# Another first stage for one transformer block: whole-row token tiles, another load order, another pass order

## The chip, the cores and the metric

The kernel runs on one core of one Trainium2 chip. Its time is the device time of one execution in microseconds (us). The kernel before takes 1711.54 us, the median of three runs (1708.84 to 1712.44). The profile is of one more execution, which took 1710.46 us.

## The reference: what is computed

One layer works on 256 latent tokens `x` and 256 context tokens `ctx`, all float32, model width 2048. The first stage computes the beginning of it: a modulated RMS norm of both token sets, times the columns of `w_in` that give keys and values.

```
m_lat = adaln(c,     w_ada, b_ada)      # silu(c) @ w_ada + b_ada, six chunks of 2048: shift, scale, ...
m_ctx = adaln(c_ctx, w_ada, b_ada)
hc = rms_norm(ctx, norm1_g) * (1 + m_ctx[1]) + m_ctx[0]
h  = rms_norm(x,   norm1_g) * (1 + m_lat[1]) + m_lat[0]
pc = hc @ w_in[:, :3072]                # keys and values of the context tokens
p  = h  @ w_in                          # keys, values, queries and gates of the latent tokens
...                                     # grouped-query and differential attention, gates, two projections
x  = x + gate * ((silu(h2 @ w_ff_gate) * (h2 @ w_ff_up)) @ w_ff_down)
```

## The kernel before, in words

**Numbers.** Every float32 product is made of three passes on TensorE: each operand is split into a high part (rounded, `hi`) and a low part (the rest, `lo`), and hi x hi, hi x lo and lo x hi are added in PSUM. For a weight tile ScalarE makes the high part (line 227, tile `whi`) and VectorE, once GpSimd, the low part (line 229, tile `wlo`).

**Keys and values in steps.** The 2048 rows of `w_in` are worked off in six steps of 1, 1, 2, 4, 4 and 4 row tiles of 128. A step needs the shift and scale of its rows for both token sets. `ada_cond` makes them from the array `ada_t`, the columns of `w_ada` in an order that suits the steps: it loads 512 KB pieces (line 282, tile `wada`), multiplies them on TensorE with the conditioning vectors (line 290), copies the sums out (line 294, `asb`), turns them (line 299, `atp`) and ends on VectorE (lines 302 to 309). Step 0 and step 1 have four such pieces each, step 2 has eight.

**Step 0, where the change lies.** There are four groups of 128 tokens: 2 and 3 are `x`, 0 and 1 are `ctx`. They are worked in the order 2, 3, 0, 1. For each one `row_norm` sums the squares of a 128x2048 row block (four quarters: two on ScalarE at line 128, two on VectorE at line 130), adds up the partial sums (line 133) and takes the power -1/2 on GpSimd (line 134). `row_scale` multiplies the first 128 columns by the result (line 139). `mod_first` turns these 128 columns on TensorE (line 355, `xtp`), and makes the modulated high part on ScalarE (line 360) and the low part on VectorE (lines 361 and 362). `kv_first` multiplies with five column groups of 512 of the first weight rows: groups 2 and 3, then 4 and 5, then 0, so 15 matmuls per token group, 60 in all (lines 370, 371 and 373), and copies the sums out (lines 378 and 380). Column group 1 follows apart (`group_1`, lines 233 to 235). `keep_busy` puts transposes of the identity into TensorE's queue (line 345) that compute nothing of use.

**Then.** `spread_rstd` spreads the four norms over the partitions (line 152). From step 1 on, rows come turned from DRAM (`tok_t`, line 162), `modulated` makes both parts (lines 331 to 335), and the matmuls of lines 233 to 235 run in one stream. Attention, the output projection and the feed-forward part follow, with the same three-pass matmuls.

**What sets the order.** The code is written in the order of the work, and a list scheduler of the language orders each engine's instructions from it by its own estimates; `issue_after` holds an instruction behind another. All large loads are issued by one queue, SP, strictly in order. An SP load waits until its buffer is free: weights and `wada` pieces share a ring of seven 4 KB-per-partition buffers (`wraw`), taken in order. At most eight loads are under way, since the ninth reuses the semaphore of the first.

## Time and profile before

| | before |
|---|---|
| median of three runs | 1711.54 us (1708.84 to 1712.44) |
| the profiled execution | 1710.46 us |
| its span from first to last instruction | 1708.7 us |
| TensorE busy (PE) | 1682.3 us, 98% |
| TensorE weight load (PEld) | 1354.0 us, 79% |
| VectorE busy (DVE) | 1148.3 us, 67% |
| ScalarE busy (ACT) | 769.8 us, 45% |
| GpSimd busy (POOL) | 202.2 us, 12% |
| DMA | 413.15 MB, mean 242 GB/s |
| granted TensorE clock | 0.998 of full |

Of the profiled time 1.8 us lie outside the span. A row of a timeline gives the start in us from the beginning of the span, the time busy, the engine, the line, the operation, the tile written and the tiles read, how many instructions were merged, and in brackets how long the engine had been idle and what ended it. "SPq" rows are load issues. Float32 matmuls of `wada` and transposes are run as two instructions each, so that counts in the trace are twice those of the program there.

### The profile page before, as it was taken

The numbers are of one execution on the slowest core, as the hardware profiler recorded it, in microseconds if no ns is written. First come the engines' busy times: TensorE is split into PE (matmuls) and PEld (weight loads), VectorE is DVE, ScalarE is ACT, GpSimd is POOL, SyncE is SP. The second block draws the span as 40 slices with busy tenths as digits, with TensorE's granted clock in tenths as the row PEclk, the third lists the DMA queues.
The fourth block names the chain that finished last, engine by engine and source line by source line (L and its number), as shares of the span: only waits on it lengthen the run. The fifth ranks groups of instructions, "written<-read, shape, count | busy, mean of one in ns | idle before, by whom it ended". The sixth has DMA issues, their size and how long they took to land.

```text
span 1708.7 us, 21517 instructions
## 1 busy us (share of the span) xinstructions
PE 1682.3 (98%) x7889; PEld 1354.0 (79%) x7889; DVE 1148.3 (67%) x1459; ACT 769.8 (45%) x1045; POOL 202.2 (12%) x296
## 2 busy tenths in 40 slices
...
GB/s 285 304 295 267 265 333 175 210 259 259 251 179 220 223 224 282 231 246 206 244 272 237 295 173 222 222 271 264 266 270 265 266 275 255 237 219 191 219 205 91
DMA packets 181291, 413.15 MB, mean 242 GB/s; under 512 B 15008, under 2 KB 16240, under 8 KB 180928
## 3 DMA queue, kind: packets, MB, share of 16 engines
...
## 4 chain that ended last, share of the span: by engine, by line
PE 87%; DVE 5%; DMA 3%; ACT 2%; issue 2%; POOL 1%; SPq 0%; ACTq 0%; DVEq 0%; POOLq 0%
PE mm L233 26%; PE mm L234 26%; PE mm L235 26%; PE ada L290 2%; DVE wlo L229 1%; PE ptp L764 1%; ACT whi L227 1%; DMA wraw<-in_w_in_dram 1%; PE o L785 1%; PE s L740 1%; ACT p L689 1%; DMA fturn<-turn_d 0%; DMA tok<-in_x_dram 0%; DVE nr L479 0%; DMA gate_d<-gate 0%
## 5 line engine op out<-in xcount | busy, mean ns | idle before, releaser
L229 DVE TENSOR_TENSOR wlo<-wraw,whi 128x1024 fp32r<-128x1024 f32 x497 | 606.6, 1222 | 420.2 <-ACT whi L227 419.3
L227 ACT CAST whi<-wraw 128x1024 fp32r<-128x1024 f32 x498 | 523.0, 1051 | 729.1 <-PE mm L235 606.3
L234 PE MATMUL mm<-wlo,hT 128*128 128x512 f32 x684 | 266.2, 389 | 0.8 <-DVE wlo L229 0.8
L233 PE MATMUL mm<-whi,hT 128*128 128x512 f32 x684 | 266.2, 389 | 0.0
L235 PE MATMUL mm<-whi,hT 128*128 128x512 f32 x684 | 266.1, 389 | 0.0
L233 PE MATMUL mm<-whi,xT 128*128 128x512 f32 x630 | 251.8, 403 | 1.5 <-ACT xT L334 0.7
L234 PE MATMUL mm<-wlo,xT 128*128 128x512 f32 x630 | 247.1, 392 | 1.1 <-DVE wlo L229 1.0
L235 PE MATMUL mm<-whi,xT 128*128 128x512 f32 x630 | 246.1, 391 | 0.0
L431 DVE SCALAR_TENSOR_TENSOR ada<-wada,vt,ada 128x1024 f32<-128x1024 f32 x120 | 152.1, 1278 | 0.0
L234 PEld LDWEIGHTS mm<-wlo,hT 128*128 128x128 f32 x684 | 128.4, 188 | 27.6 <-DVE wlo L229 1.1
L233 PEld LDWEIGHTS mm<-whi,hT 128*128 128x128 f32 x684 | 128.4, 188 | 26.9 <-ACT whi L227 0.3
L235 PEld LDWEIGHTS mm<-whi,hT 128*128 128x128 f32 x684 | 128.4, 188 | 26.8
L233 PEld LDWEIGHTS mm<-whi,xT 128*128 128x128 f32 x630 | 117.7, 188 | 39.2 <-issue 13.1
L234 PEld LDWEIGHTS mm<-wlo,xT 128*128 128x128 f32 x630 | 118.5, 188 | 26.1 <-DVE wlo L229 2.9
L235 PEld LDWEIGHTS mm<-whi,xT 128*128 128x128 f32 x630 | 118.3, 188 | 25.2
L233 PE MATMUL mm<-whi,fT 128*128 128x512 f32 x354 | 137.5, 388 | 0.5 <-DVE y L1083 0.5
L234 PE MATMUL mm<-wlo,fT 128*128 128x512 f32 x354 | 137.3, 388 | 0.0
L235 PE MATMUL mm<-whi,fT 128*128 128x512 f32 x354 | 137.3, 388 | 0.0
L233 PEld LDWEIGHTS mm<-whi,fT 128*128 128x128 f32 x354 | 66.4, 188 | 15.3 <-issue 0.8
L235 PEld LDWEIGHTS mm<-whi,fT 128*128 128x128 f32 x354 | 66.4, 188 | 13.8
L234 PEld LDWEIGHTS mm<-wlo,fT 128*128 128x128 f32 x354 | 66.5, 188 | 13.5
L233 PE MATMUL mm<-whi,oT 128*128 128x512 f32 x192 | 75.9, 396 | 0.0
...
## 6 DMA issues: line engine op xcount, KB each, us to landing
wraw<-in_w_in_dram SPq DMA_DIRECT2D x159, 512.0 KB, 5.0
wada<-in_w_ada_dram SPq DMA_DIRECT2D x128, 512.0 KB, 4.7
wraw<-in_w_ff_gate_dram SPq DMA_DIRECT2D x88, 512.0 KB, 4.4
wraw<-in_w_ff_up_dram SPq DMA_DIRECT2D x88, 512.0 KB, 5.3
wraw<-in_w_ff_down_dram SPq DMA_DIRECT2D x88, 512.0 KB, 4.4
wada<-in_ada_t_dram SPq DMA_DIRECT2D x64, 512.0 KB, 5.9
wraw<-in_w_br_a_dram SPq DMA_DIRECT2D x32, 512.0 KB, 5.0
wraw<-in_w_out_dram SPq DMA_DIRECT2D x32, 512.0 KB, 5.3
```

The source lines that it names most:

```text
L227: last_hi.append(nc.scalar.copy(out=hi[:, 0:nk], in_=raw[:, 0:nk]))
L229: last_lo.append((by or nc.vector).tensor_tensor(out=lo[:, 0:nk], in0=raw[:, 0:nk], in1=hi[:, 0:nk].bitcast(F32), op=ALU.subtract))
L233: nc.tensor.matmul(ps, lhsT=ah, rhs=wh, start=first, stop=False, skip_group_check=skip)
L234: nc.tensor.matmul(ps, lhsT=ah, rhs=wl, start=False, stop=False, skip_group_check=skip)
L235: return nc.tensor.matmul(ps, lhsT=al, rhs=wh, start=False, stop=last, skip_group_check=skip)
L290: last_pe[0] = nc.tensor.matmul(aps[32 * g:32 * g + 32, 0:ncol], lhsT=cst[:, k, :], rhs=rhs, start=(k < 4), stop=(k >= NKT - 4))
L431: nc.vector.scalar_tensor_tensor(out=dst, in0=wt, scalar=sc[:, 0, kt:kt + 1], in1=dst, op0=ALU.mult, op1=ALU.add)
L689: nc.scalar.activation(out=p, in_=sp, func=AF.Exp, bias=mx, accum_out=rs)
L740: nc.tensor.matmul(sps[i], lhsT=qT[rows, x, hh, tk * P:(tk + 1) * P], rhs=kT["b", grp][y][rows, hh, :], start=(n == 0), stop=(n == 2))
L764: nc.tensor.transpose(out=tp[:, kt * P:(kt + 1) * P], in_=p[:, kt * P:(kt + 1) * P], identity=ident)
L785: nc.tensor.matmul(op[:, 0:BV], lhsT=pT[:, kt, :], rhs=vb[:, kt, hh * BV:(hh + 1) * BV], start=(kt == 0), stop=(kt == 3))
```

## The change

The change touches the first stage alone.

- A token group's 2048 columns lie in one tile per group, loaded as two pieces of 128x1024; before, a quarter of the columns of all groups shared a tile and each group came in four pieces of 128x512.
- Token group 2 is loaded ahead of the four `wada` pieces of step 0; the weights of column groups 2 to 5 follow them, then group 3, the weights of column group 0, and the context groups.
- The squares: ScalarE takes the middle 1024 columns in one instruction, VectorE the first and the last 512. All but the first 512 columns are written over in place.
- Group 2 is normed and turned before the conditioning of step 0 is computed; the turning is a step of its own (`turn_first`). `keep_busy` stands at three places with six transposes each, before at two with eight and six.
- All low parts of weights are made on VectorE. Group 2's own modulation stands ahead of the weight splits on VectorE.
- In `kv_first` the pass with the low part of the weights comes last; before, the pass with the low part of the tokens did.
- For group 3 the leftover column group 0 of group 2 comes first.

**Place 1: SP's queue at the start.** `head` holds the conditioning vectors, `wada` the conditioning pieces, `tok` the token tiles, `wraw` the weights, `tok_t` the turned tokens of the later steps. Before:

```order
L88 DMA head<-in_head_dram 80x128
L282 DMA wada<-in_ada_t_dram 128x1024 x4
L101 DMA tok_92<-in_x_dram 128x512
L101 DMA tok_93<-in_x_dram 128x512
L101 DMA tok_94<-in_x_dram 128x512
L101 DMA tok_95<-in_x_dram 128x512
L208 DMA wraw<-in_w_in_dram 128x1024 x2
```

and, behind the context tokens:

```order
L216 DMA wraw<-in_w_in_dram 128x2x512
L162 DMA tok_t_408<-in_x_t_dram 128x2x384
L162 DMA tok_t_408<-in_ctx_t_dram 128x2x384
L282 DMA wada<-in_ada_t_dram 128x1024 x4
L208 DMA wraw<-in_w_in_dram 128x1024
```

Now:

```order
L102 DMA tok_92<-in_x_dram 128x1024 x2
L282 DMA wada<-in_ada_t_dram 128x1024 x4
L208 DMA wraw<-in_w_in_dram 128x1024 x2
L102 DMA tok_185<-in_x_dram 128x1024 x2
L208 DMA wraw<-in_w_in_dram 128x512
L102 DMA tok_190<-in_ctx_dram 128x1024 x2
L102 DMA tok_193<-in_ctx_dram 128x1024 x2
L216 DMA wraw<-in_w_in_dram 128x2x512
L282 DMA wada<-in_ada_t_dram 128x1024 x4
L208 DMA wraw<-in_w_in_dram 128x1024
L162 DMA tok_t_389<-in_x_t_dram 128x2x384
L162 DMA tok_t_389<-in_ctx_t_dram 128x2x384
```

Group 2's tokens moved ahead of step 0's four pieces, and step 1's four pieces ahead of the turned tokens.

**Place 2: TensorE from the last matmuls of token group 3 into the first context group.** `xT` is the modulated token part of `x`, `cT` that of `ctx`. Before:

```order
L373 MATMUL mm<-whi,xT_216 128x512 x4
L355 MATMUL xtp<-ident,tok_92 128x128
L370 MATMUL mm<-whi,xT_216 128x512
L371 MATMUL mm<-wlo,xT_216 128x512
L373 MATMUL mm<-whi,xT_216 128x512
L370 MATMUL mm<-whi,xT_216 128x512
L371 MATMUL mm<-wlo,xT_216 128x512
L373 MATMUL mm<-whi,xT_216 128x512
L370 MATMUL mm<-whi,cT 128x512
L371 MATMUL mm<-wlo,cT 128x512
```

Now:

```order
L374 MATMUL mm<-whi,xT_205 128x512
L375 MATMUL mm<-whi,xT_205 128x512
L377 MATMUL mm<-wlo,xT_205 128x512
L290 MATMUL ada<-wada,cst 32x128
L351 MATMUL xtp<-ident,tok_190 128x128
L290 MATMUL ada<-wada,cst 32x128 x8
L374 MATMUL mm<-whi,cT 128x512 x4
L290 MATMUL ada<-wada,cst 32x128 x4
L375 MATMUL mm<-whi,cT 128x512 x2
L377 MATMUL mm<-wlo,cT 128x512 x2
```

Thirteen of the 32 conditioning matmuls of step 1 moved from behind the context groups into the first of them, nine of these ahead of its first matmul; further on, 16 of them stand in and behind the second context group and 3 behind `group_1`. Of step 2's matmuls of 256 columns, 16 now stand ahead of the stream of step 1; before, eight did.

**Place 3: VectorE from the modulation of token group 3 on.** `vb` and `ka` are copies of sums out of PSUM. Before:

```order
L130 SCALAR_TENSOR_TENSOR junk,sums<-tok_93 128x512
L361 TENSOR_SCALAR hx<-xtp,mod_162,mod_134 128x128
L229 TENSOR_TENSOR wlo<-wraw,whi 128x512
L362 TENSOR_TENSOR xT_216<-hx,xT_216 128x128
L130 SCALAR_TENSOR_TENSOR junk,sums<-tok_95 128x512
L133 TENSOR_REDUCE sums<-sums 128x1
L139 TENSOR_SCALAR tok_92<-tok_92,sums 128x128
L378 COPY vb_106<-mm 128x512
```

Now:

```order
L365 TENSOR_SCALAR hx<-xtp,mod_177,mod_149 128x128
L366 TENSOR_TENSOR xT_205<-hx,xT_205 128x128
L229 TENSOR_TENSOR wlo<-wraw,whi 128x512
L133 SCALAR_TENSOR_TENSOR junk,sums<-tok_190 128x512
L382 COPY ka_101<-mm 128x512
L133 SCALAR_TENSOR_TENSOR tok_190,sums<-tok_190 128x512
L133 SCALAR_TENSOR_TENSOR junk,sums<-tok_193 128x512
L136 TENSOR_REDUCE sums<-sums 128x1
L382 COPY vb_105<-mm 128x512
L139 TENSOR_SCALAR tok_190<-tok_190,sums 128x128
```

Ahead of the scaling of the first context group (line 139) there now stand two copies of sums and one square of the second context group. Further on, inside step 2, two transposes of the conditioning stand about 24 matmuls later on TensorE; behind that every engine's order is the same in both kernels.

The diff:

```diff
--- before.py
+++ after.py
@@ -89,17 +89,20 @@
     warm = small("warm", 1)
     nc.scalar.activation(out=warm, in_=neghalf[:, 0:1], func=AF.Silu)
     sums = tab.tile([P, 24], F32, name="sums")
-    ssq, r_tok = sums[:, 0:20].rearrange("p (i q) -> p i q", i=4), sums[:, 20:24]
+    ssq, r_tok = sums[:, 0:16].rearrange("p (i q) -> p i q", i=4), sums[:, 20:24]
     nc.gpsimd.memset(sums, EPS)
-    tok_in = [big_tile(f"tok{q}").rearrange("p (i c) -> p i c", i=4) for q in range(4)]
+    tok_in = {}
     def load_tokens(src, i):
-        for q in range(4):
-            nc.sync.dma_start(out=tok_in[q][:, i, :], in_=src[0, i % 2 * P:(i % 2 + 1) * P, q * CG:(q + 1) * CG])
-
+        tok_in[i] = big_tile(f"tok{i}")
+        for h in range(2):
+            nc.sync.dma_start(out=tok_in[i][:, h * 2 * CG:(h + 1) * 2 * CG],
+                              in_=src[0, i % 2 * P:(i % 2 + 1) * P, h * 2 * CG:(h + 1) * 2 * CG])
+
+    load_tokens(t["x"], 2)
     nc.scalar.activation(out=head[0:32, :], in_=head[0:32, :], func=AF.Silu)
     hps = tp_ps("hps")
     nc.tensor.transpose(out=hps[:, 0:80], in_=head, identity=ident[0:80, 0:80])
@@ -120,22 +123,19 @@
         last_pow.append(nc.gpsimd.tensor_tensor(out=r, in0=r, in1=neghalf[:, 0:n], op=ALU.pow))
         return r
-    def row_norm(i):
-        for q in range(4):
-            xt = tok_in[q][:, i, :]
-            junk = scratch("junk", tag="p", bufs=4)
-            if q % 2 == 0:
-                nc.scalar.activation(out=junk, in_=xt, func=AF.Square, scale=D ** -0.5, accum_out=ssq[:, i, q:q + 1])
-            else:
-                nc.vector.scalar_tensor_tensor(out=junk, in0=xt, scalar=1.0 / D, in1=xt, op0=ALU.mult, op1=ALU.mult,
-                                               accum_out=ssq[:, i, q:q + 1])
+    def row_norm(i, late=None):
+        xt = tok_in[i]
+        mid, end = xt[:, CG:3 * CG], xt[:, 3 * CG:]
+        with tc.issue_after(late[0].ins) if late else nullcontext():
+            nc.scalar.activation(out=mid, in_=mid, func=AF.Square, scale=D ** -0.5, accum_out=ssq[:, i, 0:1])
+        with tc.issue_after(late[1].ins) if late else nullcontext():
+            for n, (src, dst) in enumerate(((xt[:, 0:CG], scratch("junk", tag="p", bufs=4)), (end, end))):
+                nc.vector.scalar_tensor_tensor(out=dst, in0=src, scalar=1.0 / D, in1=src, op0=ALU.mult, op1=ALU.mult,
+                                               accum_out=ssq[:, i, 1 + n:2 + n])
         r = r_tok[:, i:i + 1]
         nc.vector.tensor_reduce(out=r, in_=ssq[:, i, :], axis=AX.X, op=ALU.add)
         last_pow.append(nc.gpsimd.tensor_tensor(out=r, in0=r, in1=neghalf[:, 0:1], op=ALU.pow))
-        return r
-
-    def row_scale(i, r):
-        xt = tok_in[0][:, i, 0:P]
+        xt = xt[:, 0:P]
         nc.vector.tensor_scalar(out=xt, in0=xt, scalar1=r, scalar2=None, op0=ALU.mult)
     r_of = []
@@ -216,7 +216,7 @@
         nc.sync.dma_start(out=raw[:, 0:nk], in_=src[r0:r0 + nk * P, c0:c0 + CG].rearrange("(k p) c -> p k c", p=P))
         return split_w(raw, nk, in_big)
-    def split_w(raw, nk, in_big=False, late=None, by=None):
+    def split_w(raw, nk, in_big=False, late=None):
         if in_big:
             both = big_tile("wbig", F32R).rearrange("p (h k c) -> p h k c", h=2, c=CG)
             hi, lo = both[:, 0], both[:, 1]
@@ -226,7 +226,7 @@
         with tc.issue_after(late[0].ins) if late else nullcontext():
             last_hi.append(nc.scalar.copy(out=hi[:, 0:nk], in_=raw[:, 0:nk]))
         with tc.issue_after(late[1].ins) if late else nullcontext():
-            last_lo.append((by or nc.vector).tensor_tensor(out=lo[:, 0:nk], in0=raw[:, 0:nk], in1=hi[:, 0:nk].bitcast(F32), op=ALU.subtract))
+            last_lo.append(nc.vector.tensor_tensor(out=lo[:, 0:nk], in0=raw[:, 0:nk], in1=hi[:, 0:nk].bitcast(F32), op=ALU.subtract))
         return hi, lo
     def mm3(ps, ah, al, wh, wl, first, last, skip=False):
@@ -344,6 +344,12 @@
             for _ in range(n):
                 nc.tensor.transpose(out=idle[:, 0:P], in_=ident, identity=ident)
+    turned_first = {}
+
+    def turn_first(tok):
+        turned_first[tok] = tp_ps("xtp")[:, 0:P]
+        last_pe[0] = nc.tensor.transpose(out=turned_first[tok], identity=ident, in_=tok_in[tok][:, 0:P])
+
     def mod_first(tok):
         k0, nk = steps[0]
@@ -351,14 +357,12 @@
         w, c0 = (0, (tok - 2) * P) if tok >= 2 else (1, tok * P)
         if k0 not in cT_of:
             cT_of[k0] = big_tile("cT", F32R).rearrange("p (h k c) -> p h k c", h=2, c=CTX)
-        tp = tp_ps("xtp")
-        last_pe[0] = nc.tensor.transpose(out=tp[:, 0:P], identity=ident, in_=tok_in[0][:, tok, 0:P])
+        tp = turned_first[tok]
         hx = scratch("hx")[:, 0:P]
         v = xT.tile4(0) if w == 0 else cT_of[k0]
         hi, lo = [v[:, x, 0, c0:c0 + P] for x in range(2)]
-        with tc.issue_after(last_hi[-1].ins):
-            first_hi.append(nc.scalar.activation(out=hi, in_=tp[:, 0:P], func=AF.Identity, scale=scale[:, 0, w:w + 1], bias=shift[:, 0, w:w + 1]))
-        nc.vector.tensor_scalar(out=hx, in0=tp[:, 0:P], scalar1=scale[:, 0, w:w + 1], scalar2=shift[:, 0, w:w + 1], op0=ALU.mult, op1=ALU.add)
+        first_hi.append(nc.scalar.activation(out=hi, in_=tp, func=AF.Identity, scale=scale[:, 0, w:w + 1], bias=shift[:, 0, w:w + 1]))
+        nc.vector.tensor_scalar(out=hx, in0=tp, scalar1=scale[:, 0, w:w + 1], scalar2=shift[:, 0, w:w + 1], op0=ALU.mult, op1=ALU.add)
         last_first.append(nc.vector.tensor_tensor(out=lo, in0=hx, in1=hi.bitcast(F32), op=ALU.subtract))
         firsts[tok] = hi, lo
@@ -368,9 +372,9 @@
         for cg in cgs:
             wh, wl = ws0[cg]
             nc.tensor.matmul(ps[cg], lhsT=hi, rhs=wh, start=True, stop=False)
-            nc.tensor.matmul(ps[cg], lhsT=hi, rhs=wl, start=False, stop=False)
+            nc.tensor.matmul(ps[cg], lhsT=lo, rhs=wh, start=False, stop=False)
         for cg in cgs:
-            last_pe[0] = nc.tensor.matmul(ps[cg], lhsT=lo, rhs=ws0[cg][0], start=False, stop=True)
+            last_pe[0] = nc.tensor.matmul(ps[cg], lhsT=hi, rhs=ws0[cg][1], start=False, stop=True)
         for cg in cgs:
             nm, idx = kv_of[cg]
             dst = acc[nm][idx][:, tok * CG:(tok + 1) * CG]
@@ -559,37 +563,38 @@
     BATCH = ((), (1, 4), (0, 1, 2, 3), (0, 1, 2, 3), (0, 1, 2, 3), ())
     steps = STEPS
+    row_norm(2)
+    turn_first(2)
+    keep_busy(6)
     drain(ada_cond(*steps[0]))
     ws0 = {}
-    def hold(cg, by=None):
+    def hold(cg, late=None):
         n = 2 if cg else 1
-        wh, wl = split_w(raws[cg], n, by=by)
+        wh, wl = split_w(raws[cg], n, late=late)
         for j in range(n):
             ws0[cg + j] = wh[:, j], wl[:, j]
-    raws = {}
-    for tok in (2, 3, 0, 1):
-        load_tokens(t["x"] if tok >= 2 else t["ctx"], tok)
-        if tok == 2:
-            for cg in (2, 4):
-                raws[cg] = load_raw(0, cg * CG)
-            with tc.issue_after(last_asb[-1].ins):
-                hold(2)
-        elif tok == 3:
-            raws[0] = load_raw(0, 0, 1)
-    for tok, todo in ((2, ((2, (2, 3)), (2, (4, 5)))), (3, ((3, (2, 3)), (3, (4, 5)), (2, (0,)), (3, (0,)))),
+    raws = {cg: load_raw(0, cg * CG) for cg in (2, 4)}
+    load_tokens(t["x"], 3)
+    raws[0] = load_raw(0, 0, 1)
+    for tok in (0, 1):
+        load_tokens(t["ctx"], tok)
+    keep_busy(6)
+    mod_first(2)
+    hold(2, (last_asb[-1], last_first[-1]))
+    hold(4, (first_hi[-1], last_first[-1]))
+    kv_first(2, (2, 3))
+    kv_first(2, (4, 5))
+    keep_busy(6)
+    for tok, todo in ((3, ((2, (0,)), (3, (2, 3)), (3, (4, 5)), (3, (0,)))),
                       (0, ((0, (2, 3)), (0, (4, 5)), (0, (0,)))), (1, ((1, (2, 3)), (1, (4, 5)), (1, (0,))))):
-        r = row_norm(tok)
-        row_scale(tok, r)
-        if tok == 2:
-            keep_busy(8)
+        row_norm(tok, (last_hi[-1], last_lo[-1]))
+        with tc.issue_after(last_pe[0].ins):
+            turn_first(tok)
         mod_first(tok)
-        if tok == 2:
-            keep_busy(6)
-        if tok >= 2:
-            with tc.issue_after(first_hi[-1].ins):
-                hold(*((4, nc.gpsimd) if tok == 2 else (0,)))
+        if tok == 3:
+            hold(0, (first_hi[-1], last_first[-1]))
         for of in todo:
             kv_first(*of)
     group_1 = kv_group(0, 2, 1, True)
```

## The prediction

> **What bounds the kernel now.** I read first the busy time of each engine by stretches of the program. The columns are the stretch, its length, the busy time of TensorE (PE), its weight load, VectorE (DVE), ScalarE (ACT) and GpSimd (POOL), each with instructions, then the granted clock, the DMA share and GB/s.
>
> ```profile
> 0.00:31.18 31.18, 18.48 (x114) 12.91 (x115) 13.56 (x36) 13.96 (x32) 5.37 (x14) 0.89 0.93 346
> 31.18:48.49 17.31, 15.89 (x135) 10.03 (x133) 10.40 (x25) 7.43 (x16) 0.55 (x1) 1.00 0.46 164
> 48.49:110.00 61.51, 61.51 (x327) 41.96 (x328) 43.60 (x72) 15.47 (x24) 9.54 (x32) 1.00 0.88 321
> 110.00:1708.60 1598.60, 1586.38 (x7317) 1289.08 (x7315) 1080.71 (x1329) 732.95 (x976) 186.74 (x249) 1.00 0.74 238
> ```
>
> From 48.49 us on TensorE is the bound: it is busy all the time up to 110, and behind that all but 12.2 us of 1598.6. Before 31.18, where the first matmul of a context group stands, it is idle for 12.7 us, and part of the rest runs at half clock. So the change is worth what it takes off the time until the dense stream, if the stream then does not wait.
>
> Next I read the timeline of the first token groups, in order of time, to see which wait ends last.
>
> ```profile
> 10.80 0.63 ACT L128 ACTIVATE junk<-tok 128x512 f32<-128x512 f32 x1 [7.92 <-DMA tok<-in_x_dram]
> 14.12 0.27 ACT L294 COPY asb<-ada 128x128 f32<-128x128 f32 x1 [1.22 <-PE ada L290]
> 14.28 1.05 ACT L227 CAST whi<-wraw 128x1024 fp32r<-128x1024 f32 x1
> 15.36 0.17 DVE L302 TENSOR_REDUCE mod<-atp 128x2 f32<-128x8 f32 x1 [1.56 <-PE atp L299]
> 15.83 0.16 DVE L309 SCALAR_TENSOR_TENSOR mod<-mod,vt 128x2 f32<-128x2 f32 x1
> 15.91 1.22 DVE L229 TENSOR_TENSOR wlo<-wraw,whi 128x1024 fp32r<-128x1024 f32 x1
> 16.17 0.46 ACT L360 ACTIVATE xT<-xtp,mod,mod 128x128 fp32r<-128x128 f32 x1 [0.84 <-PE xtp L355]
> 17.06 0.41 DVE L361 TENSOR_SCALAR hx<-xtp,mod,mod 128x128 f32<-128x128 f32 x1
> 17.50 0.29 DVE L362 TENSOR_TENSOR xT<-hx,xT 128x128 fp32r<-128x128 f32 x1
> 17.64 2.38 POOL L229 TENSOR_TENSOR wlo<-wraw,whi 128x1024 fp32r<-128x1024 f32 x1 [3.12 <-ACT whi L227]
> 17.71 2.87 DVE L130 SCALAR_TENSOR_TENSOR junk<-tok 128x512 f32<-128x512 f32 x1
> 20.08 0.74 PE L371 MATMUL mm<-wlo,xT 128*128 128x512 f32 x2 [1.21 <-POOL wlo L229]
> 20.66 0.63 PE L373 MATMUL mm<-whi,xT 128*128 128x512 f32 x2
> 21.09 0.69 DVE L378 COPY vb<-mm 128x512 f32<-128x512 f32 x1 [0.51 <-PE mm L373]
> 21.70 0.68 DVE L130 SCALAR_TENSOR_TENSOR junk<-tok 128x512 f32<-128x512 f32 x1
> 22.73 0.55 POOL L134 TENSOR_TENSOR sums<-sums,neghalf 128x1 f32<-128x1 f32 x1 [2.71 <-DVE sums L133]
> 23.66 0.47 PE L355 MATMUL xtp<-ident,tok 128*128 128x128 f32 x1 [2.37 <-DVE tok L139]
> 24.53 0.61 ACT L227 CAST whi<-wraw 128x512 fp32r<-128x512 f32 x1
> ```
>
> The reader sees a chain: tokens at 10.8, behind them on ScalarE the copy of the conditioning sums, which is why scale and shift are ready only at 16.0; GpSimd's low part until 20.0, on which TensorE waits; and one VectorE square of 2.87 us beside it where the next takes 0.68. Token group 3 is turned only at 23.66.
>
> **Part 1, the loads.** SP's issues, and the time from issue to landing of single ones (KB, us):
>
> ```profile
> 1.21 0.41 SPq L282
> wada<-in_ada_t_dram SPq DMA_DIRECT2D x1, 512.0 KB, 3.6
> 2.61 0.44 SPq L282
> wada<-in_ada_t_dram SPq DMA_DIRECT2D x1, 512.0 KB, 6.0
> 3.09 7.62 DMA tok<-in_x_dram
> ```
>
> The first `wada` piece lands at 1.21 + 3.6 = 4.8, the fourth at 2.61 + 6.0 = 8.6: 1.28 per 512 KB. The first token quarter lands at 10.7, 2.1 behind, where 256 KB at that rate need 0.64: 1.4 us are lost at the first read of `x`. In the new order this may come again or not; I take half, 0.7, and keep 0 and 1.4 for the range. Then group 2's tokens land at 5.5 and 6.8, `wada` at 8.1 to 11.9, the weights at 13.2 and 14.5, group 3 at 15.7 and 17.0, the last context piece at 22.8, and step 1's pieces at 25.4, 26.6, 27.9 and 29.2.
>
> **Part 2, token group 2.** Its norm and transpose now end while `wada` still comes, at no cost. After the last piece: 0.5 for eight conditioning matmuls, 0.3 the copy, 0.4 the transpose, 0.6 from line 302 to 309: scale ready at 13.7. ScalarE splits the first weights until 14.3 and makes the high part until 14.75; VectorE makes hx and the low part until 15.5, then two low weight parts of 1.22, until 17.95. The last pass ends at 18.4; before, 20.66 + 0.63 = 21.3. Taking the 2.38 off GpSimd adds 1.22 to VectorE, inside this chain. The other pass order is what lets four of six passes run ahead of the low weight parts. Writing in place I cost at nothing: same shapes, the same engines.
>
> **Part 3, group 3 and the first context group.** VectorE goes on from 17.95: two squares of 0.75 (0.68 and the read of the sum), a sum of 0.15, GpSimd 0.85 (0.55 and 0.15 each way), a copy beside it, scaling 0.3, transpose 0.3: turned at 21.05. High part 0.46, then the high part of column group 0 (0.61), which stands first on TensorE: matmuls from 22.15. VectorE then needs, before the context group is scaled, hx and low part 0.7, low weight part 0.7, three squares of 0.75, one copy of 0.7, a sum 0.15 and GpSimd's 0.85, from 21.5 to 26.9; the second copy hides under GpSimd. Scaling 0.3, transpose 0.3 and high part 0.46 give 28.0. TensorE's 18 matmuls of 0.23 end at 26.3, and step 1's second piece, which nine conditioning matmuls ahead of the context group need, lands at 26.6: VectorE's chain decides.
>
> The clock can add to it:
>
> ```profile
> 15.62:22.45 6.83, 4.46 (x22) 2.85 (x20) 6.19 (x11) 4.83 (x11) 2.38 (x1) 1.00 1.05 387
> 22.45:29.27 6.82, 5.06 (x12) 3.84 (x13) 3.41 (x11) 2.62 (x8) 1.10 (x2) 0.50 1.05 394
> 25.48 0.43 PE mm L371
> 36.27 0.23 PE mm L370
> ```
>
> The last two rows are single matmuls of the chain of waits. From 22.45 to 29.27 the clock was granted at one half, and matmuls came 0.43 apart instead of 0.23. TensorE had been idle for at most 2.4 us at a time before. The change leaves it idle from about 19.2 (18.4 and six transposes) to 22.15 but for one transpose, so the half clock may come again. If it holds half as long, 3.4 us from 22.45, 1.7 are lost: the 14 matmuls whose sums the second copy needs end at 22.15 + 3.2 + 1.7 = 27.1, the copy at 27.8, and the context group starts at 28.9. I take **28.4**, between 28.0 and 28.9; with the full 1.4 and the half clock 29.7, with neither 27.3. The gain here is 31.18 - 28.4 = **2.8**.
>
> The Trainium skill, "TensorE: Matmul & The Clock Gate" (HAM oscillation), warns of idle gaps of over about 3.4 us. By it the gap of some 2 us here is harmless and 28.0 would stand, a sum better by 0.4. The trace does not agree: gaps of at most 2.4, in a stretch with 4.46 of 6.83 us busy, were followed by the half clock.
>
> **Part 4, from there to the stream.**
>
> ```profile
> 35.54 0.50 PE L370 MATMUL mm<-whi,cT 128*128 128x512 f32 x1 [0.55 <-ACT cT L360]
> 43.94 1.30 PE L290 MATMUL ada<-wada,cst 128*32 128x128 f32 x40
> 46.45 0.33 PE L299 MATMUL atp<-ident,asb 128*128 128x128 f32 x1 [0.16 <-ACT asb L294]
> 46.70 1.06 PE L290 MATMUL ada<-wada,cst 128*32 128x256 f32 x14
> 48.49 0.50 PE L233 MATMUL mm<-whi,xT 128*128 128x512 f32 x1 [0.72 <-ACT xT L334]
> ```
>
> Before, this takes 48.49 - 31.18 = 17.3. Nine of the 32 conditioning matmuls of step 1 are done earlier, in idle time: 9 x 0.062 (1.30 for 20) = 0.56. The gap of 0.55 at the second context group is filled by eight others. The gap of 0.16 goes, and 0.1 of the 0.72. Sum 1.4. That eight more matmuls of step 2 (1.06 for eight) stand ahead only moves them. Their pieces need a buffer that the low part of `group_1`'s weight frees: 3.8 for the first context group's matmuls, 0.8 to the second's high part, 1.4 to its low part and 1.2, so at 35.6; the third piece behind it lands 3.6 + 2 x 1.28 = 6.2 later, at 41.8, and is used at about 44. This cover of 2 us is what keeps it free; later, it costs what it is late. Bounds 0.9 and 1.9. The gain is **1.4**.
>
> **Part 5, the stream.** I cost it at nothing.
>
> ```profile
> SPq L282 <- PE ada L290: 32.8, 10, 7.6
> PE mm L233 <- DVE vb L414: 0.7, 1, 0.7
> ```
>
> The first row, of the waits of SP up to 120 us, says that loads waited on TensorE to free their buffers; the second is the only wait of TensorE between 60 and 200, and not on a load. So loads move with TensorE.
>
> **Sum.** 2.8 + 1.4 = 4.2 us off the profiled 1710.46, to 1706.3. The median of the three runs is 1.08 above that execution; off 1711.54 it is **1707.3**. With the ends of parts 3 and 4 the gain is 2.4 to 5.8: 1705.7 to 1709.1.
>
> **The rivals.**
>
> *No delay and full clock.* The token rows come without the 1.4 and the clock stays up. The context group starts at 27.3: gain 3.9 + 1.4 = 5.3, 1706.2. For it: 4 KB rows instead of 2 KB, denser matmuls. Against: the idle time from 19.2 on. Chance 0.18. (The skill's clock rule, named in part 3, would give this clock.)
>
> *A wait for step 1's pieces takes the place of the chain.*
>
> ```profile
> wada<-in_ada_t_dram SPq DMA_DIRECT2D x1, 512.0 KB, 9.2
> 31.18 0.40 PE L370 MATMUL mm<-whi,cT 128*128 128x512 f32 x1
> ```
>
> The second piece, issued at 22.2, landed at 31.4. Since nine conditioning matmuls now stand ahead of the context groups, such a landing would start them at 31.7: 0.5 lost, 1.4 won, gain 0.9, 1710.6. Against: 768 KB of turned tokens no longer stand ahead of it, 1.9 at the rate of part 1. Chance 0.10.
>
> *The stream gives it back.* DMA is at a share of 0.88 up to 110; if the loads cannot come earlier, TensorE waits for them and nothing is left: 1711.5. Against it stands the first row of part 5. Chance 0.10.
>
> *Slower: the clock stays at half.* If the gap from 19.2 to 22.15 and the wait behind group 3 keep the clock at half until 42.9, two stretches of 6.8 more than before, matmuls from 28.4 on take twice as long: 14.5 / 2 = 7.2 lost, and 1.0 in group 3; less 4.2, 4.0 slower: 1715.5. It decides when the second stretch is also at half. Against: before, dense matmuls brought the clock back within one stretch. Chance 0.05.
>
> **How the numbers follow.** The forecast holds 0.55, the rivals 0.18, 0.10, 0.10 and 0.05; 0.02 is for what I don't see. 0.2% is 3.4 us, about what a measurement of this kernel tells from no change, so faster begins below 1708.1. Four fifths of the forecast (0.45), the first rival and half of the unseen are faster: 0.64. A fifth of the forecast, the second and the third rival are the same: 0.30. The fourth and the rest are slower: 0.06. The range goes from 1704.0, the best ends (1705.7) less 1.7 for the spread of the runs, to 1711.8, which takes in the second and third rival.
>
> **What would show it.** Right: scale and shift at about 13.7 and group 2's last pass at 18.4 (part 2); no VectorE square of 2.87; group 3 turned at 21; the first matmul on `cT` at 28.4, waiting for ScalarE and not for `wada` (part 3); the stream from about 45.3, with 16 matmuls of step 2 ahead of it (part 4). Wrong: a half clock behind 30, TensorE waits on `wada` or `wraw` between 45 and 110, or a first matmul on `cT` later than 30.

## The result, and the profile after

The changed kernel takes 1706.77 us (median of 22 runs, 1704.99 to 1711.31), the kernel before, measured beside it, 1709.41 us (22 runs, 1707.16 to 1712.44). The ratio is 0.9986, 95% interval 0.998 to 0.9992: by it 2.4 us faster, between 1.4 and 3.4; the two medians lie 2.64 apart. It is a gain, and it is smaller than the 0.2% that the prediction set as the bound of "faster". The profiled execution took 1708.76 us with a span of 1707.0.

Busy time by stretches, after; columns as in the prediction.

```profile
0.00:30.97 30.97, 19.53 (x136) 13.28 (x136) 14.07 (x41) 13.69 (x25) 2.99 (x13) 0.94 0.94 358
30.97:48.58 17.61, 17.32 (x136) 10.27 (x132) 9.50 (x23) 7.73 (x15) 0.59 (x1) 1.00 0.70 219
```

The first context matmul stands at 30.97 instead of 31.18, the stream of step 1 at 48.58 instead of 48.49. But 16 matmuls of step 2 now stand ahead of it instead of eight (1.06 us), so the stream is reached 48.49 + 1.06 - 48.58 = 1.0 earlier in work. The span is 1.7 shorter. The other 0.7 arose behind the start of the stream, where TensorE was idle for 11.5 us in this execution and for 12.3 before; the runs do not show why.

The chain of waits after, from the conditioning on (start, length, engine, tile and line):

```profile
10.27 0.41 PE xtp L351
10.68 1.28 PE idle L345 x6
11.96 1.44 PE ada L290 x24
13.40 0.42 PE atp L299
13.82 1.30 PE ada L290 x22
15.12 0.59 PE idle L345 x4
```

TensorE's own queue is the chain here, not the last `wada` piece, which landed at 12.15. Conditioning matmuls come 1.44 / 24 = 0.06 apart on average, and 1.30 / 22 = 0.06 to the end. The last of them started before 14.85, where the clock became full: keep-busy transposes took 1.28 / 6 = 0.21 each ahead of that and 0.59 / 4 = 0.15 behind it. So all of step 0's conditioning ran at half clock, and six keep-busy transposes stand among it. The timeline after, the rows that answer to those of before:

```profile
16.26 0.16 DVE L309 SCALAR_TENSOR_TENSOR mod<-mod,vt 128x2 f32<-128x2 f32 x1
16.97 0.50 PE L374 MATMUL mm<-whi,xT 128*128 128x512 f32 x1 [0.93 <-ACT xT L364]
17.61 2.35 DVE L229 TENSOR_TENSOR wlo<-wraw,whi 128x1024 fp32r<-128x1024 f32 x2
19.88 0.69 DVE L133 SCALAR_TENSOR_TENSOR junk<-tok 128x512 f32<-128x512 f32 x1
20.37 0.62 PE L377 MATMUL mm<-wlo,xT 128*128 128x512 f32 x2
22.46 0.33 PE L351 MATMUL xtp<-ident,tok 128*128 128x128 f32 x1 [0.81 <-DVE tok L139]
28.95 0.69 DVE L382 COPY vb<-mm 128x512 f32<-128x512 f32 x1 [1.63 <-PE mm L377]
29.56 0.28 DVE L139 TENSOR_SCALAR tok<-tok,sums 128x128 f32<-128x128 f32 x1
30.97 0.73 PE L374 MATMUL mm<-whi,cT 128*128 128x512 f32 x2
48.58 0.51 PE L233 MATMUL mm<-whi,xT 128*128 128x512 f32 x1 [0.29 <-ACT xT L334]
```

The VectorE square of 2.87 is gone (0.69). The instruction that ends the scale and shift (line 309) starts at 16.26, even later than before (15.83), and takes 0.16, group 2's last pass ends at 21.0 (before 21.3), and group 3 is turned (its transpose starts) 5.5 behind the first matmul on `xT`; before it was 7.0. Then VectorE waits 1.63 for TensorE, which runs at half clock. Windows of after (the third number from the end is the granted clock):

```profile
18.27:21.68 3.41, 3.19 (x16) 2.14 (x15) 3.31 (x8) 2.29 (x5) 0.15 (x1) 1.00 1.03 418
21.68:25.09 3.41, 1.58 (x6) 1.17 (x7) 2.39 (x6) 2.27 (x5) 0.40 (x1) 1.00 1.04 400
25.09:28.51 3.42, 3.42 (x9) 2.65 (x8) 2.15 (x8) 1.86 (x4) 0.55 (x1) 0.50 1.02 408
```

In the execution before, two stretches in a row were at half (22.45 to 29.27); in this one, one. From 23.84 to the first context matmul TensorE had no gap: at half clock it is the bound there.

Three questions follow: why scale and shift came 2.7 later than forecast (16.26 + 0.16 against 13.7), what the half clock costs and goes by, and why the way to the stream got no shorter. The working theory at first was that TensorE at half clock and its useless transposes set the first 16 us, and a second stretch at half the next 14. The rivals: the loads, GpSimd's or VectorE's share, the order of the passes.

### The profile page after: what moved, and what is told of

The parts are those of the page before. It is cut to its first block, busy times and chain, and to the rows that moved or that the text cites. A ratio compares the mean times of both kernels' runs of the same rounds, so it can differ in the third digit from the quotient of the medians.

```text
span 1707.0 us, 21494 instructions
## 1 busy us (share of the span) xinstructions
PE 1683.8 (99%) x7893; PEld 1354.3 (79%) x7893; DVE 1146.4 (67%) x1460; ACT 768.8 (45%) x1037; POOL 201.0 (12%) x295
## 4 chain that ended last, share of the span: by engine, by line
PE 88%; DVE 5%; DMA 2%; ACT 2%; issue 2%; POOL 0%; SPq 0%; DVEq 0%; ACTq 0%
PE mm L233 27%; PE mm L234 27%; PE mm L235 27%; PE ada L290 2%; DVE wlo L229 1%; DMA wraw<-in_w_in_dram 1%; PE ptp L769 1%; PE o L790 1%; ACT whi L227 1%; PE s L745 1%; ACT p L694 1%; DVE nr L483 0%; DMA wada<-in_ada_t_dram 0%; DMA gate_d<-gate 0%; DVE mx L691 0%
## 5 line engine op out<-in xcount | busy, mean ns | idle before, releaser
L234 PEld LDWEIGHTS mm<-wlo,hT 128*128 128x128 f32 x684 | 128.4, 188 | 27.3 <-DVE wlo L229 0.5
L234 PEld LDWEIGHTS mm<-wlo,fT 128*128 128x128 f32 x354 | 66.5, 188 | 13.7
```

Of the source, the lines that this page charges most:

```text
L234: nc.tensor.matmul(ps, lhsT=ah, rhs=wl, start=False, stop=False, skip_group_check=skip)
```

## The experiments

In what follows "line 309" is the start of the instruction that ends the scale and shift (0.16 long), "C" the first context matmul, "S" the start of the stream of step 1. Each kernel is the changed one with the edit shown, unless it says otherwise. Where there is no ratio, there is one time only, and the trace is what is read.

**The first keep-busy transposes.**

```
     turn_first(2)
-    keep_busy(6)
     drain(ada_cond(*steps[0]))
```

> The changed kernel without the first six keep-busy transposes, which stand on TensorE between the transpose of token group 2 and the conditioning matmuls of step 0. Theory A: TensorE itself, at half clock and never idle from 8.4 to 15.1 us, makes scale and shift late, and the six transposes (10.68 to 11.96 in the changed kernel) are in that chain: without them the last VectorE step of the conditioning (line 309) starts at about 15.0 instead of 16.26, the first matmul on x (line 374) at about 15.7 instead of 16.97, and the first matmul on a context group about 1 us before 30.97. Rival B: the last piece of the conditioning weights is what is waited for, so nothing moves (line 309 at 16.2 to 16.3). Rival C: without the transposes the clock comes up later, so that line 309 starts at 15 but the matmuls behind it run 0.43 apart for longer and the context group starts no earlier than 30.9.

Line 309 at 14.83 instead of 16.26, C at 29.53 instead of 30.97, S at 47.36 instead of 48.58. Median 1706.98, ratio to before 0.9985 (0.9976 to 0.9995), level with the change. So the six transposes cost 1.43 on the chain, as the row of 1.28 in after said, and the gain stays on the way to C (a stretch of 3.41 us at half clock, from 23.68, fell ahead of C here too); a time of the whole kernel cannot tell 1.2 us.

**Transposes ahead of the conditioning.**

```
+    warm_ps = mm_ps("idle")
+    for _ in range(18):
+        nc.tensor.transpose(out=warm_ps[:, 0:P], in_=ident, identity=ident)
...
     turn_first(2)
-    keep_busy(6)
     drain(ada_cond(*steps[0]))
```

> The changed kernel without the first six keep-busy transposes, and with 18 of them in the idle time of TensorE ahead of the first conditioning matmul (from about 3.5 us on). Theory A: 18 transposes at half clock last 4.5 us and bring the clock up before the conditioning matmuls, which then come 0.03 apart instead of 0.06; scale and shift wait for their last piece (12.15): line 309 at 13.7 to 14.2 instead of 16.26, first matmul on x at 14.5 to 15.2, first context matmul 2 us before the changed kernel's, at 28.0 to 29.0. Rival B: transposes do not count for the clock (the Trainium skill, TensorE: Matmul & The Clock Gate, Part 4: PE-mode transpose), so only their removal counts, as in the run without the first six: line 309 at 14.8, the context group at 29.5.

Windows of this kernel, on the boundaries at which its clock was granted. Ahead of the first record the view prints 1.00 for the clock; the pace of the matmuls there is that of the half clock.

```profile
1.44:4.85 3.41, 2.02 (x10) 2.05 (x11) 0.00 (x0) 1.09 (x3) 0.42 (x3) 1.00 0.69 205
4.85:8.26 3.41, 2.19 (x11) 1.78 (x9) 1.65 (x6) 1.15 (x2) 0.00 (x0) 1.00 1.00 378
```

The clock rose only at 15.09, line 309 came at 15.96, the ratio is 0.9995 (0.9986 to 1.0004). I read this as the rival's case, that transposes do not count for the clock. That reading fell later: the transposes ran from 2.99 to 7.04 and filled neither of the first two windows (2.02 and 2.19 of 3.41). That line 309 came 1.1 later than in the run before has another reason: the transpose of group 2 now stood ahead of all conditioning matmuls, and waited for VectorE until 9.54, so that they began at 9.94, though their first piece had landed at 8.43.

**Real matmuls instead.** 24 matmuls of the identity by itself at the same place, the other keep-busy transposes made into such matmuls, and:

```
-    turn_first(2)
-    keep_busy(6)
-    drain(ada_cond(*steps[0]))
+    ada_first = ada_cond(*steps[0])
+    next(ada_first)
+    with tc.issue_after(last_pe[0].ins):
+        turn_first(2)
+    drain(ada_first)
```

> The changed kernel, with 24 real matmuls of the identity by itself (128x128) ahead of the conditioning, where TensorE has nothing to do; the first six keep-busy transposes are gone, the other twelve are such matmuls too, and the transpose of token group 2 stands behind the first 16 conditioning matmuls. Theory A (TensorE at half clock is what the first conditioning waits for, and transposes do not count for the clock while matmuls do): the clock is full by about 10 us, the conditioning matmuls come 0.03 apart instead of 0.06, scale and shift (line 309) are ready at 13.7 to 14.3 instead of 16.26, the first matmul on x stands at 14.5 to 15.0, the first context matmul at 27 to 28.5, and the time is about 2 us under that of the changed kernel. Theory B (the kind of operation does not matter, or the matmuls are too few): line 309 not before 14.8, as it was without the six transposes alone, the first context matmul at 29 or later, and a time within 1 us of the changed kernel.

```profile
5.33:8.74 3.41, 3.41 (x18) 3.41 (x17) 1.80 (x7) 1.15 (x2) 0.15 (x1) 1.00 0.99 392
2.99 8.31 PE L111 MATMUL idle<-ident 128*128 128x128 f32 x48
11.23 1.08 PE L293 MATMUL ada<-wada,cst 128*32 128x128 f32 x32
```

The clock was full from 8.74 and the conditioning matmuls 0.03 apart, as theory A said. But the 24 matmuls are run as 48 instructions (a transpose is one, not two as the part on the profile before has it), last until 11.2, and hold the conditioning back, whose first piece had landed at 8.3: line 309 at 15.36. C 29.13, S 46.58. Ratio 0.9989 (0.998 to 0.9997). Half of theory A came: the clock rose, but the fillers cost in the queue what it won.

**More transposes, or none, behind group 2.** Twelve instead of six at the third `keep_busy`:

> The changed kernel with twelve instead of six keep-busy transposes behind token group 2's matmuls (idle time of TensorE between about 21.6 and 22.5). Theory A: too little work in the stretch up to 25.1 brought the clock to half from 25.09 to 28.51, and 0.8 us more of transposes keep it up: no row at half clock, the 18 matmuls of token group 3 0.23 apart, the first context matmul at about 30.0 instead of 30.97. Rival B: transposes do not count for the clock, as the Trainium skill says in TensorE: Matmul & The Clock Gate (Part 4: PE-mode transpose): the half clock stays and the context group starts at 30.9 to 31.2.

No half clock from 14.27 to 618, C at 29.09, S at 46.71; one time, 1706.97. In the window from 21.10 to 24.51 TensorE was busy for 2.21 us, 0.92 of it with these transposes; six, done by about 21.35, would have left some 1.5 us (an estimate), which is 0.45 of the window, and in after a window with 0.46 was followed by the half clock. So here the six more probably held the clock. But four other executions with only six there (those with 18 transposes ahead, with the old pass order, with the old load order and with `r_all` together) stayed at full clock as well. And none at all, the three calls taken out:

> The changed kernel without any of its 18 keep-busy transposes. Theory A (they do nothing for the clock and only stand in TensorE's queue): the clock rises as before at 14 to 16 us, line 309 at about 14.8, the first context matmul at 28.5 to 29.5 (full clock) or 30 to 31 (with a stretch of 3.4 us at half), and the time is level with the changed kernel or up to 1.5 us under it. Theory B (they hold the clock up): line 309 at 14.8, but half clock for 6.8 us or more between 17 and 40, the first context matmul at 32 or later, and a time at least 1 us above the changed kernel.

```profile
16.32:19.73 3.41, 3.41 (x9) 2.50 (x10) 3.31 (x7) 2.00 (x4) 0.00 (x0) 0.50 1.04 420
23.14:26.56 3.42, 3.42 (x10) 2.64 (x9) 2.69 (x7) 2.03 (x5) 0.00 (x0) 0.50 1.04 406
```

Line 309 at 14.67, but two stretches of 3.41 at half with one at full between them; C at 29.79. Ratio 0.999 (0.9981 to 0.9999): neither better nor clearly worse than the change. Both theories have a part: the transposes cost 1.4 at the first place, and without any the clock fell twice in this execution, where after and its other edited kernels had one such stretch or none. One execution does not show that this is the rule.

**The same idea in the kernel before.** Its 14 transposes as real matmuls, `nc.tensor.matmul(idle[:, 0:P], lhsT=ident, rhs=ident, ...)`:

> The kernel before, whose 14 keep-busy transposes are real matmuls of the same size in the same places. Theory A (half of what the change won is the clock: 6.8 us at half before, 3.4 or none after): the half clock from 22.45 to 29.27 goes or is at most 3.4 us long, the first context matmul stands at 28.5 to 29.8 instead of 31.18, and the time is 1 to 2.5 us under the kernel before. Theory B (the change won by its order, and the half clock costs nothing because other work sets the end): with or without the half clock the first context matmul stays at 30.5 to 31.5 and the time within 0.7 us of the kernel before.

```profile
15.38 2.56 PE idle L345 x12
24.71:28.12 3.41, 1.76 (x4) 1.28 (x5) 2.19 (x7) 1.79 (x5) 0.55 (x1) 0.50 1.05 388
28.12:31.53 3.41, 3.41 (x9) 2.63 (x9) 1.16 (x5) 0.86 (x3) 0.55 (x1) 0.50 1.03 409
```

Slower: 1713.36, ratio 1.0021 (1.0012 to 1.0031). The matmuls stood in TensorE's queue, with only the transpose of group 2 among them, until the first matmul on `xT` (19.18 instead of 16.68; the first row, of the chain of waits, has 12 of these 24 instructions), C came at 33.37, and the half clock stayed 6.8 us long. Both theories were wrong: fillers that stand ahead of ready work cost what they last, and they do nothing for windows that begin when they are through.

**GpSimd's part.** One of the two low weight parts back on GpSimd (`split_w` with the engine as an argument, group 3's squares no longer behind it):

> The changed kernel with the low part of the weights of column groups 4 and 5 on GpSimd again, as in the kernel before. Theory A: with low-weight passes last, a slow GpSimd (2.4 us) is hidden: token group 2's last pass still ends at 20.9 to 21.3, and VectorE, freed of 1.2 us, has token group 3 turned about 1 us before 22.46. Rival B: VectorE's squares beside GpSimd take 2.9 us instead of 0.7, as one did before, and group 3 is turned 1 us or more later than 22.46.

```profile
17.84 3.14 POOL L229 TENSOR_TENSOR wlo<-wraw,whi 128x1024 fp32r<-128x1024 f32 x1 [8.85 <-ACT whi L227]
18.65 2.88 DVE L133 SCALAR_TENSOR_TENSOR junk<-tok 128x512 f32<-128x512 f32 x1
21.04 0.73 PE L377 MATMUL mm<-wlo,xT 128*128 128x512 f32 x2 [0.59 <-POOL wlo L229]
```

The slow square is back, 2.88 beside 3.14 of GpSimd. It ended 0.55 behind GpSimd's instruction (21.53 after 20.98), as one did before the change (20.58 after 20.02), so it looks like a wait and not like slow work. And group 3 is turned at 23.42 with line 309 at the same place (16.17): 1.0 later. C at 31.90, S at 49.50. This part of the change is worth about 0.9 there; one time, 1708.0, is too little to see it in.

**The order of the passes.** The low weight part in the middle again:

```
-            nc.tensor.matmul(ps[cg], lhsT=lo, rhs=wh, start=False, stop=False)
+            nc.tensor.matmul(ps[cg], lhsT=hi, rhs=wl, start=False, stop=False)
...
-            ... matmul(ps[cg], lhsT=hi, rhs=ws0[cg][1], start=False, stop=True)
+            ... matmul(ps[cg], lhsT=lo, rhs=ws0[cg][0], start=False, stop=True)
```

> The changed kernel with the passes of the first matmuls in the old order again (high x low weights second, low tokens x high weights last). Theory A: VectorE's chain sets the start of the context groups, so the pass order matters little: token group 2's last pass ends 0.3 to 0.9 us later relative to its first matmul than in the changed kernel (4.0 us there), and token group 3 is turned 5.2 to 5.7 us behind that first matmul, as it is there (5.49). Rival B: the later passes hold back the copies of sums that stand on VectorE ahead of group 3, and group 3 is turned 6.2 us or more behind the first matmul.

```profile
18.08 0.74 PE L375 MATMUL mm<-wlo,xT 128*128 128x512 f32 x2 [0.24 <-DVE wlo L229]
21.66 0.33 PE L351 MATMUL xtp<-ident,tok 128*128 128x128 f32 x1 [0.59 <-DVE tok L139]
```

TensorE waits a little for the low part, but group 3 is turned 5.49 behind the first matmul on `xT`, just as in after: VectorE's chain decides, and the passes run beside it. C at 29.09, without a half stretch. One time, 1705.4.

**The order of the loads.** Group 2's tokens behind the four `wada` pieces, as before:

```
-    load_tokens(t["x"], 2)
     nc.scalar.activation(out=head[0:32, :], in_=head[0:32, :], func=AF.Silu)
...
+    drain(ada_cond(*steps[0]))
+    load_tokens(t["x"], 2)
     row_norm(2)
     turn_first(2)
     keep_busy(6)
-    drain(ada_cond(*steps[0]))
```

> The changed kernel with token group 2 loaded, normed and turned behind the conditioning of step 0, as before, all else as changed. Theory A: the early tokens brought nothing, since the conditioning was then late by TensorE's slow clock and the transposes in its way: the first matmul on x comes at 15.5 to 17.0, as in the changed kernel (16.97), and the time is within 0.1% of the changed kernel's, 0.9986 of the kernel before. Rival B: the early load is what the change lives on: the first matmul at 18 or later and a ratio of 0.9995 or more.

Line 309 at 14.95, the first matmul on `xT` at 17.41 (after 16.97), C at 28.49, S at 46.20, no half clock behind 17.90. Ratio 0.9987 (0.9975 to 1.0). So the whole kernel shows no worth of the new load order. The first matmul, outside both ranges, does not show it either, since the edit also moved six transposes:

```profile
14.99 2.77 PE L344 MATMUL idle<-ident 128*128 128x128 f32 x12
```

Twelve transposes at half clock stood right ahead of the first matmul on `xT` and held it until 17.41, when its `xT` had long been made (15.69). Against the run without the first six transposes, line 309 is level (14.95 and 14.83), and group 3 is turned at 21.41 instead of 21.02. What the tokens win, the conditioning loses, it seems: the loads are under way all the time (a DMA share of about 1.0 in every window of after shown above), and here the last `wada` piece landed at 8.70 and the tokens at 12.15, in after the tokens at 7.02 and `wada` at 12.15.

**The norm ahead of the copies.** In the loop over groups the norm of the next group stands ahead of the matmuls of the last:

```
+    row_norm(3, (last_hi[-1], last_lo[-1]))
     for tok, todo in ((3, ...
-        row_norm(tok, (last_hi[-1], last_lo[-1]))
...
+        if tok != 1:
+            row_norm(0 if tok == 3 else 1, (last_hi[-1], last_lo[-1]))
         for of in todo:
```

> The changed kernel with the norm of the next token group written ahead of the matmuls of the present one, so that on VectorE the scaling of context group 0 stands ahead of the copy of token group 3's sums instead of behind it. Theory A: in the changed kernel the scaling (29.56) waited behind a copy that waited for TensorE (from 27.3 to 28.95); ahead of it the first context matmul comes at most 6.0 us behind the first matmul of token group 3 with the clock at half (7.13 in the changed kernel), and TensorE's own 18 matmuls become what is waited for. Rival B: TensorE's matmuls are the bound there already, so the context group starts 6.8 us or more behind when the clock is at half.

```profile
27.63 0.29 DVE L139 TENSOR_SCALAR tok<-tok,sums 128x128 f32<-128x128 f32 x1 [0.44 <-POOL sums L137]
29.51 0.39 PE L377 MATMUL mm<-wlo,xT 128*128 128x512 f32 x1
30.56 0.73 PE L374 MATMUL mm<-whi,cT 128*128 128x512 f32 x2
```

The scaling no longer waits behind a copy (27.63 instead of 29.56), but C only moves to 30.56, 6.67 behind the first matmul of group 3 (23.89), between the two theories: with a stretch at half clock the last of group 3's own matmuls stands at 29.51, and TensorE is the bound there, as rival B has it. One time, 1712.9, with 6.8 us of half clock at 622 in its trace as well.

**The four `r_all` matmuls together.**

```
+        with tc.issue_after(last_pe[0].ins):
             for g in range(4):
                 nc.tensor.matmul(ps[32 * g:32 * g + 32, :], lhsT=ones, rhs=diag, ...)
```

> The changed kernel with the four matmuls of the norm spreading (r_all, four column groups of 32) held behind the last matmul of the second context group, so that they stand together; the step-2 conditioning matmuls then also come in multiples of four. Theory A: matmuls for different column groups run side by side only when they stand together; one of them apart cost 0.86 and the other three 0.99 in the changed kernel, against 0.99 for four before. Together they should take about 1.0 in all, and the stream of step 1 (line 233 behind the wait for xT) should start 0.8 to 1.2 earlier relative to the first context matmul: 16.4 to 16.8 behind it instead of 17.61. Rival B: the first of them fills a wait for the low part of the second context group, so nothing is won (17.4 to 17.7).

After, TensorE's rows:

```profile
37.32 1.02 PE L152 MATMUL r_all<-diag,ones 128*32 128x512 f32 x2
38.27 0.73 PE L375 MATMUL mm<-whi,cT 128*128 128x512 f32 x2
40.31 1.06 PE L152 MATMUL r_all<-diag,ones 128*32 128x512 f32 x6
41.30 0.33 PE L299 MATMUL atp<-ident,asb 128*128 128x128 f32 x1
```

and with the edit:

```profile
28.26 0.65 PE L291 MATMUL ada<-wada,cst 128*32 128x128 f32 x16
28.88 1.20 PE L375 MATMUL mm<-whi,cT 128*128 128x512 f32 x4
41.77 1.06 PE L153 MATMUL r_all<-diag,ones 128*32 128x512 f32 x8
42.77 0.33 PE L300 MATMUL atp<-ident,asb 128*128 128x128 f32 x1
45.72 0.62 PE L291 MATMUL ada<-wada,cst 128*32 128x256 f32 x2 [0.36 <-DMA wada<-in_ada_t_dram]
```

One `r_all` matmul (two instructions) by itself holds TensorE for 38.27 - 37.32 = 0.95, the other three for 0.99, all four together for 1.00. The split that the changed order made costs 0.94. Of it S - C keeps only 0.14 (17.47 against 17.61): at the end TensorE now waits 0.36 for a piece of step 2, and one more of step 2's matmuls and a transpose stand ahead. The rest of the 0.94 is not accounted for. C at 28.88 is early because no stretch at half fell behind group 2 in this execution (its windows there have 0.60 and more). Ratio 0.9985 (0.9976 to 0.9995).

**What the clock goes by.** With these traces one can lay each execution's grid of 3.41 us, on which its clock changes, over the whole span, and take the share of each window in which TensorE was busy, transposes counted. Fourteen traces (before, after and the twelve runs) have 6958 windows, without the last two of each, in which the program ends:

```
full clock, half in the next window : 14 windows, shares 0.08 to 0.475
full clock, full in the next window : lowest shares 0.473, 0.483, 0.499, 0.507, 0.52
half clock, full in the next window : 28 windows, shares 0.916 to 1.00
half clock, half in the next window : highest shares 0.863, 0.845, 0.816, 0.788
```

The clock falls after one window with less than about 0.48, and rises after one with more than some 0.9; between 0.863 and 0.916 there is no case. The lower bound is not sharp: in the last us of after the clock fell behind a window with 0.495. One window rose at 0.925 of which 0.15 were other than transposes (in the run with the old load order); so transposes count. The last run was made to test that, and what it would give:

```
+    warm_ps = mm_ps("idle")
+    for _ in range(24):
+        nc.tensor.transpose(out=warm_ps[:, 0:P], in_=ident, identity=ident)
...
+    ada_first = ada_cond(*steps[0])
+    next(ada_first)
+    with tc.issue_after(last_pe[0].ins):
+        turn_first(2)
+    keep_busy(4)
+    drain(ada_first)
...
     kv_first(2, (4, 5))
-    keep_busy(6)
+    keep_busy(12)
...
+                    with tc.issue_after(after_kv[0].ins) if k0 == 1 else nullcontext():
...
+            if br == "a" and u == 0 and i == 1:
+                keep_busy(12)
```

The norm ahead of the copies and the `r_all` matmuls together are as in the two runs above; `after_kv` is the last matmul of the first context group, and the last two lines stand in the function that turns the attention weights.

> The changed kernel with 24 transposes of the identity ahead of the conditioning (18 in an earlier run ended at 7.04), the first six keep-busy transposes gone and the transpose of group 2 with four others behind the first 16 conditioning matmuls; 12 transposes instead of six behind group 2; the norm of each next group ahead of the matmuls of the last; the four r_all matmuls together; the conditioning of step 1 behind the first context group; 12 transposes in the gap of 1.9 to 3.1 us at about 618. Theory A (the clock of a stretch of 3.41 us goes by how much of the stretch before TensorE was busy, transposes too; and at full clock the first context matmul waited for step 1's second conditioning piece): full clock from a place between 6.4 and 10 us with only transposes behind it, line 309 at 13.6 to 14.2, the first matmul on x at 14.3 to 14.9, the first context matmul at 26.0 to 27.5, ahead of that piece's landing at about 28.5; no half clock at 618; the stream of step 1 from 43.8 to 45.5; the time 3 to 5 us under the changed kernel. Theory B (transposes do not count for the clock): it rises at 12 us or later, line 309 at 14.6 or later, a stretch at half clock between 20 and 30; the time within 2 us of the changed kernel. Theory C (the clock as in A, but the loads set the stream): the first context matmul at 26.0 to 27.5, the stream not before 46, since step 2's pieces land no earlier; 1 to 2.5 us under the changed kernel.

```profile
4.11:7.52 3.41, 3.41 (x18) 3.41 (x17) 1.59 (x6) 0.56 (x1) 0.00 (x0) 1.00 0.99 383
3.01 4.99 PE L111 MATMUL idle<-ident 128*128 128x128 f32 x24
12.19 0.64 PE L295 MATMUL ada<-wada,cst 128*32 128x128 f32 x16 [0.53 <-DMA wada<-in_ada_t_dram]
13.99 0.16 DVE L314 SCALAR_TENSOR_TENSOR mod<-mod,vt 128x2 f32<-128x2 f32 x1
18.95 0.69 DVE L136 SCALAR_TENSOR_TENSOR tok<-tok 128x512 f32<-128x512 f32 x1 [0.35 <-DMA tok<-in_x_dram]
20.68 1.53 PE L350 MATMUL idle<-ident 128*128 128x128 f32 x12 [1.64 <-ACT kb L389]
28.80 1.19 PE L379 MATMUL mm<-whi,cT 128*128 128x512 f32 x4 [0.55 <-ACT cT L369]
46.99 0.50 PE L237 MATMUL mm<-whi,xT 128*128 128x512 f32 x1 [1.01 <-ACT xT L339]
973.50:976.91 3.41, 1.48 (x9) 1.03 (x8) 2.69 (x6) 1.69 (x3) 0.97 (x2) 1.00 0.94 320
976.91:980.32 3.41, 3.41 (x12) 2.81 (x12) 3.41 (x5) 1.16 (x2) 0.00 (x0) 0.50 0.35 137
```

A window with nothing but transposes, full clock from 7.52, line 309 at 13.99: theory A on the clock holds and theory B falls. No half clock followed until 976. TensorE now waits 0.53 for the last `wada` piece, so the loads are what sets line 309 here. But C came at 28.80, not at 26 to 27.5. The first matmul on `xT` stood at 15.00, and group 3 was turned 7.05 behind it instead of 5.5, for two reasons. Its second token piece landed at 18.92 (17.66 in after), which made the scaling 0.9 later against that matmul (21.01). And the twelve transposes behind group 2, which had waited for a copy on ScalarE, held TensorE until 22.05, 0.75 behind the end of the scaling: fillers in the way again. And S stands at 46.99 behind a wait of 1.01, 18.2 from C. So of 2.3 us won at line 309 (against after) 2.2 are left at C and 1.6 at S, but after had a half stretch ahead of C; against the run with `r_all` together, which had none, C is only 0.1 earlier and S 0.6 later; theory C's 46 for the stream is what came, though not by its reason alone, since C was late too. Median 1706.57 against 1710.75 of before beside it, ratio 0.9976 (0.9966 to 0.9986): the fastest ratio of all kernels here, by an interval that still overlaps that of the change. Its median alone is level with that of the change (1706.77).

## Why the prediction was right or wrong

**The time.** 1707.3 was forecast, 1706.77 measured. That is closer than the working deserves, and it is luck. The forecast took 4.2 off 1711.54, the median of three runs; 22 runs put before at 1709.41. Between the medians the gain was 2.64 (2.4 by the ratio), so a base that was 2.13 too high made up for a gain that was 1.6 too high. By the ratio the change lies within 0.2%, which had a chance of 0.30 against 0.64 for faster. Of the forecast's own signs one of being wrong came, a first matmul on `cT` later than 30. Of those of being right the square of 2.87 went, and 16 matmuls of step 2 stand ahead of the stream, but every time named there was missed, by 1.5 to 3.3 us. In the two profiled executions the way to the stream got shorter by 0.2 up to C and by 0.8 behind it, where 2.8 and 1.4 were forecast. What the rest of the gain is made of no run shows: the edited kernels differ from the change by less than their intervals.

**Part 1, the loads:** right as to order and start (tokens at 5.4 and 7.0, `wada` at 8.3 to 12.15). Step 1's pieces landed at 27.3 to 31.2, 2 us behind the forecast, without harm in this execution: TensorE did not wait for one up to C.

**Part 2 failed, in one term.** From the last `wada` piece to scale and shift 1.8 was forecast, 12.15 to 16.42 = 4.3 was measured. The pieces came nearly as forecast (12.15 against 11.9), but TensorE was through with the last conditioning matmuls only at 15.1. Two things were left out. "0.5 for eight conditioning matmuls" is their price at full clock, from the row of 1.30 for 20 in part 4; at half clock the kernel before had shown twice that (two instructions for each matmul):

```profile
12.13 1.93 PE L290 MATMUL ada<-wada,cst 128*32 128x128 f32 x30
```

And the keep-busy transposes stood in the same queue for 1.28, and the transpose of group 2, "at no cost", beside them. The prediction's own row of 14.12 said that the copy waited 1.22 for TensorE; it was read as a wait on ScalarE alone. With the first six transposes gone line 309 came at 14.83, with the clock up early as well at 13.99, in a run that also moved the transpose of group 2. So the 2.7 are about 1.4 for the transposes and 0.8 for the half clock; some 0.4 is left, of which 0.25 is the landing. That VectorE takes GpSimd's part was sized right (2.35 for two, no slow square), and so was the cost of nothing for writing in place: squares of 0.69.

**Part 3** was right in mechanism: VectorE's chain turns group 3, and a half clock of 3.4 us can come behind the gap. From scale ready to the end of the turn it took 22.79 - 16.42 = 6.4, forecast 7.35; from there to C 8.2, forecast 7.35. From the start of the turn to C, after took 8.51; the seven executions of edited kernels without a half stretch there took 6.75 to 7.43, those with one of 3.41 us 8.06 to 8.51; the run with `r_all` together, which differs only further on, 6.92. So the half clock cost about 1.6 here, where 0.9 was priced and half of it taken. C at 30.97 is 2.57 late: part 2's 2.7 late, then 1.0 won and 0.8 lost.

**Part 4** was mis-sized. S - C was forecast at 16.9 and is 17.61. TensorE's idle time between the two fell from 1.42 (0.55, 0.16 and 0.72) to 0.29, more than the 0.8 that the sum took. But the new interleaving of conditioning and `r_all` matmuls with the large ones cost 0.94 in the split of `r_all`, a term that the sum did not have. With it the account closes: 17.31 - 1.13 idle - 0.56 for the nine moved + 1.06 for the eight of step 2 + 0.94 = 17.6. The run with them together won only 0.14 of that: a wait for step 2's piece (0.36) came up in its place, and part is open.

**Part 5** held: between S and the end nothing was given back (1658.4 us after; 1660.2 before, less the 1.06 for the matmuls that moved ahead of S).

**The rivals.** Of "no delay and full clock" the clock came in seven executions of edited kernels: without the half stretch C lies at 28.5 to 29.1, never at 27.3. There the second rival, the wait for step 1's second piece, is close: in the run with `r_all` together it landed at 28.27, the conditioning matmuls ahead of C start at 28.26, and C follows at 28.88. But C waited there for the high part of `cT`, which ScalarE made until 28.83, and in the last run, with this conditioning behind the first context group, C follows the turn of group 3 by 6.75 instead of 6.92. So the second rival did not come: that wait is worth 0.2 at most in these executions. The stream that gives it back and the clock that stays at half did not come either.
